# Part of a hybrid layer's elementwise work moved from VectorE and ScalarE to GpSimd

## The chip, the cores and the metric

The kernel runs on one core of a Trainium2 chip. The metric is the time of one execution on the device in microseconds (us). Five engines work side by side: TensorE (matrix products; PE in the rows, its weight loads PEld), VectorE (DVE), ScalarE (ACT), GpSimd (POOL) and SyncE (SP, which issues most transfers). Each has a queue of its own that it works off in order. TensorE's results land in PSUM, which GpSimd does not read in this kernel; all other tiles are in SBUF.

## The reference, cut to what matters

One layer of a streaming encoder runs over 512 tokens of a new stream and 64 tokens of a running one. Three of its steps matter here:

```
# state-space part, chunk by chunk
h_new = exp(last)[..., None, None] * h + einsum(w_end, x, Bk)      # decay of the state, then the update
y = (y + d_skip * xh).reshape(b, T, SSD_WIDTH) * silu(z)           # gating
y_ssd = rmsnorm(y, ssd_norm)
...
# attention part
s = where(mask, s * scale, -inf)
pr = softmax(s)                                                    # exp(s - max), divided by its sum
o = einsum(pr, keys_c) ...
x = x + concat([y_ssd, o]) @ w_out
# then a dense SwiGLU feed-forward layer
```

There are 8 state-space heads of 64 channels and 8 attention heads. All data is float32. Most products are made as three products of a high and a low half of each operand, so that many tiles come with a "high" copy (made by ScalarE) and a "low" difference (made by VectorE).

## The kernel before, in words

Tokens lie along the free dimension, channels along the 128 partitions. The work goes through input projections and convolution (to about 87 us of the profiled execution), the state-space chunks together with the gate projection and the first attention projections (87 to 144 us), attention with the first part of the output projection (144 to 218 us), the rest of the output projection (to 250 us) and then the feed-forward layer, which takes the rest.

The state-space part has five chunks: 0 to 3 of the new stream with 128 tokens each, and 4, of the running stream, with 64. `chunk_a` and `chunk_e` prepare a chunk (GpSimd's only arithmetic here is the select at line 515), `chunk_b` makes its output in the tile `xsd`, `chunk_s` the next running state `h`: a product of the old state with the decay `el` (line 569) and a sum with the update from PSUM (line 570). `gate` multiplies a chunk's part of `xsd` by `sz` (line 582); ScalarE squares the result (line 584), TensorE sums the squares over channels and ScalarE keeps the sums. When the sums of all chunks are there, `norm_y` and `cat_tile` (line 764, then `split_scaled`, lines 143 and 145) make the tiles `cat_y`, which the output projection takes.

Attention goes by pairs p of heads and blocks i of 128 queries (i = 4 is the running stream). `scores` makes a block's scores in PSUM; `soft` takes the maximum on VectorE (line 655), the exponential with its sum on ScalarE (line 656), the reciprocal of the sums on VectorE (line 657) and then scales the probabilities `pr`: head 0 of the pair on VectorE (line 662), head 1 on ScalarE (line 660). A block i of the new stream has (i + 1) x 128 keys. `turn` then transposes all blocks' probabilities through TensorE (line 694), and VectorE and ScalarE copy them back to SBUF. `pair_proj` issues, from GpSimd's queue, four transfers that bring a pair's rotary rows to the query buffer `qs` (line 616); pairs 2 and 3 reuse the buffers of pairs 0 and 1.

The order on each engine is written out: the strings `ORDER_...` give the order in which the steps are made, and the table `ISSUE` holds, for every engine, the order in which its instructions are issued, as numbers of the order in which they were made. `issue_in_order` puts it into effect. Nothing is reordered at run time.

Of the kernel before, what the change touches and what calls it, by code (L numbers as in the profile page):

```python
# [14 lines left out]
ALU = mybir.AluOpType  # L15
# [4 lines left out]
P = 128  # L20
# [34 lines left out]
def hybrid_layer_kernel(ctx: ExitStack, tc: tile.TileContext, a, o):  # L55
# [501 lines left out]
    def chunk_s(c):  # L557

        L, tk, ecp, el, xdt, bt, xw, wts = pre.pop(c)
        h = hT.pop(c)  # L560
        pst = bank("pp", f"ps_s{c}")
        for g in range(2):
            pe.matmul(pst[:, g * 256 : g * 256 + 256], bt[:L, g * P : g * P + P], xw[:L, g * 256 : g * 256 + 256], start=True, stop=True)
        hn = sd.tile([P, 512], F32, tag="hT", name=f"h_{c}", bufs=3)
        if h is None:
            act.copy(hn, pst)
        else:
            hv = lambda z: z.rearrange("p (h q) -> p h q", h=H)
            dve.tensor_tensor(hv(hn), hv(h), el.unsqueeze(2).to_broadcast([P, H, HD]), ALU.mult)
            dve.tensor_tensor(hn, hn, pst, ALU.add)  # L570
        if c == 4:
            sp.dma_start(o["ssm_sT"], hn)
        elif c == 3:
            sp.dma_start(o["ssm_pT"], hn)
        else:
            hT[c + 1] = hn

    def gate(c):
# [3 lines left out]
        dve.tensor_tensor(yv, yv, sz[:, :, tk], ALU.mult)  # L582
# [65 lines left out]
    def soft(p, i, scs, nk):  # L648
# [9 lines left out]
        for j in range(n):  # L658
            if j:
# [669 lines left out]
900-903 925-926 913-921 927-934 922-924 935 939-940 936-938 949-957 964-966 941 945-948 967-968 958-963 969 942-944
970-975 987 976-979 1003 980-986 991-993 988 1004-1005 1015-1021 1006-1014 1022-1024 994-996 1025-1026 1029-1034  # L1330
1043-1045 997-998 989 1000-1002 999 1046-1054 990 1035-1039 1059-1061 1040-1042 1062-1064 1027-1028 1075-1077
1081-1092 1055-1057 1078-1080 1093-1096 1058 1097-1104 1121-1123 1071-1072 1124-1129 1065 1068-1070 1073 1105-1107
1066-1067 1074 1130-1156 1119-1120 1229-1240 1157 1108-1114 1158 1241-1245 1253-1262 1246-1247 1115-1118 1159-1161
1176-1177 1248-1252 1263-1264 1162-1175 1265 1180 1178 1181-1183 1179 1266-1268 1277-1279 1184-1187 1190-1195
1269-1276 1196-1204 1188-1189 1205-1223 1227-1228 1224-1226 1280-1297 1301-1303 1298-1300 1304-1321 1342-1343
1348-1355 1344-1347 1322-1341 1356-1511 1572 1512-1559 1575-1576 1560-1571 1577 1596-1598 1578 1573-1574 1593
1584-1585 1579 1581-1583 1602-1604 1623-1625 1594-1595 1614 1586 1605-1606 1590-1592 1611-1613 1632-1634 1587-1589
1608-1610 1607 1580 1599-1601 1620-1622 1641 1626-1628 1647-1649 1642-1643 1615-1616 1635-1637 1617-1619 1638-1640
1653 1656 1658-1667 1644-1646 1629-1631 1650-1652 1654-1655 1668-1669 1657 1682 1694-1705 1683-1693 1670-1681
1730-1741 1706-1729 1742-1748 1754-1755 1749-1753 1756-1767 1778-1785 1768-1777 1786-1885 1898-1905 1886-1897  # L1340
1906-2017 2030-2036 2018-2029 2037-2053 2066-2084 2054-2065 2085-2089 2102-2104 2090-2101 2105-2221 2234-2236
2240-2241 2222-2233 2237 2242-2248 2238-2239 2249-2725 2738-2740 2744 2726-2737 2741 2745-2751 2742-2743 2752-3229
3242-3244 3248 3230-3241 3245 3249-3255 3246-3247 3256-3733 3746-3748 3752 3734-3745 3749 3753-3759 3750-3751
3760-4189
# [5 lines left out]
101-102 125 120 126-127 119 131-133 155 134 129 135-136 140-142 149 104 152 128 150 153 170 143-144 138 145 147 151  # L1350
154 156 137 146 174 157 178 159 171-172 187 169 160 158 161-162 176 206 163 175 183 180 164 167 165-166 168 215 181
177 188 173 189 182 184 190 195 191 179 192-194 197 185-186 224 196 204 207-209 198-203 214 205 210 288 211 225
216-218 212 220 222 219 213 226 221 223 227-228 233 229-230 234 231-232 235-236 245 255 246 237 294 256 247 239 248
257 259 258 260 240 238 264 241 261 242 263 262 307 267 243 265 244 266 249 268 270 251 269 253 250 274 252 254
275-276 289 271 290 277-279 295 286 280 282 281 287 272 297 317 291 283 318 273 298 302 299 316 300 284-285 319 303
306 292-293 296 309 312 304 326 305 310 308 313 327 362 311 328 322 301 323 314 363 330 324 320 329 315 336 321 325
364 333 367 337 331-332 365 340 338 334-335 341 344 349 339 350 345 342 346 352 351 343 355 358 366 347 359 357 348
360 356 353 361 368 377 354 370-371 369 372 375-376 373-374 382 390 378 384 383 385-386 379 389 387 380 397 388 381
393 405 395 391 396 394 392 400 399 401 398 403 402 420 406 404 408 407 409 412 410 417 414 411 413 418 462 416 421
423 419 464 425 422 424 415 433 431 426 432 429 428 427 438 430 434 469 463 436 435 437 439 442 441 443 466 440 444  # L1360
451 465 446 467-468 452-453 445 447 455 454 448 473 475 456 477 476 474 457 472 470 478 458-459 449-450 479 460 481
480 461 471 482 491 487 483 496-497 484 488 498-499 489 500-502 485-486 503 510 490 515-518 522 492 504 519 506 520
507 521 508 532-535 539 546 493-495 536 547-549 505 511-512 509 523 537 529-530 524-525 513-514 531 538 540 528 550
541 566 526 542 527 551 543 545 552 544 567-568 553-554 569 555 574 570 556-559 561 575-576 560 565 577 562 578-581
571 582-583 572 563 590-591 584 592 585-586 564 598 573 599-600 593-594 587-588 601 589 603 602 595 604-607 596 610
597 608-609 620-623 611 627 612 624 613-614 625-626 619 634-636 628 637 617 638 618 629 616 615 630 641 639 631 640
633 632 654-656 642 657 643 662 658 644-647 649 663-664 648 653 665 650 666-669 659 670-671 660 651 678-679 672 680
673-674 652 686 661 687-688 681-682 675-676 689 677 691 690 683 692-695 684 698 685 696-697 708-711 699 715 700 712
701-702 713-714 707 722-724 716 725 705 726 706 717 704 703 718 729 727 719 728 721 720 742-744 730 745 731 750 746
732-735 737 751-752 736 741 753 738 754-757 747 758-759 748 739 766-767 760 768 761-762 740 774 749 775-776 769-770  # L1370
763-764 777 765 779 778 771 780-783 772 786 773 784-785 796-799 787 803 788 800 789-790 801-802 795 810-812 804 813
793 814 794 805 792 791 806 817 815 807 816 809 808 830-832 818 833 819 839 834 820-823 825 840-841 824 829 842 826
843-846 835 847-848 836 827 855-856 849 857 850-851 828 864 837 865-866 858 838 859 852-853 867 854 869 868 860
870-873 861 876 862 874 880 875 881-883 887 884 863 885 877 886 879 878 888-898
""",
    "ACT": """
0-5 8 6-7 10 9 13 11 14 12 15 17-18 16 21 19 24 20 23 40 22 25 45 26-27 52 28-33 49-50 56 34-35 37 36 60 51 41-43
38-39 64 44 46-48 53-54 68 55 57-58 72 59 61-62 76 63 65-67 77 69-71 73 92 74-75 94 79 88 78 81 104 82 90 84 116 86-87
103 85 83 100 98 80 97 89 99 102 101 96 91 126 105 93 111 109-110 156 115 95 107-108 113 122 114 112 142 117 163 106
118-119 136 127 137 134 128 140 135 124 121 120 139 129 138 141 130 123 143 131 125 150 146 149 132 210 133 145 148  # L1380
154 152 151 147 158-159 157 144 155 160-162 153 164-165 212 170 172 171 166 168 180 186 169 181 174 187 175 173 176
189 167 190 177 227 178 192 179 193 188 182 195 194 191 183 200 196 184-185 199 201 197 213 208 215-216 202-203 219
209 204 217 234 218 198 205-206 211 214 226 220 233 221 240 207 223 242 224 222 241 229 243-244 225 271 235 230 228
231 238 237 272 232 245 236 248 239 246 249-252 247 257 255 261 254 262 256 259 263 258 278 265 253 267 266 264
268-270 260 273-277 284 280-282 285 287 283 279 293 286 291 288 290 289 302 292 294 296 295 298 300 297 301 303-304
# [123 lines left out]
```

## Time and profile before

| | before |
|---|---|
| median of 3 runs | 635.12 us (634.90 to 635.19) |
| profiled execution | 634.82 us, of which its span from first to last instruction is 633.1 us |
| granted TensorE clock, mean | 0.997 |
| TensorE busy | 622.9 us (98% of the span) |
| VectorE busy | 541.9 us (86%) |
| ScalarE busy | 400.0 us (63%) |
| GpSimd busy | 110.9 us (18%) |

The shares are averages over stages with different limits. A busy TensorE is not TensorE at its peak, since matrix products are pipelined and their ends are modelled; what holds the end is read from the chain of waits, which is followed back from the last instruction. Start times are counted from the first instruction of the span.

### The profile page before, as it was taken

How to read it: one execution, taken by the hardware profiler on the slowest of the kernel's cores; microseconds unless marked ns; L12 is line 12 of the kernel's file. 1: busy time of each engine (PE TensorE's matmuls, PEld its weight loads, DVE VectorE, ACT ScalarE, POOL GpSimd, SP SyncE). 2: the span in 40 equal slices, each digit the busy share in tenths (PEclk: the TensorE clock that was granted, in tenths of full speed). 3: DMA queues.
4: the chain of work that ended last, by engine and by line, in shares of the span. 5: the costliest groups of instructions: out<-in, count | busy, mean ns of one | idle time of the engine just before them, and what ended most of it. 6: DMA issues, size and time to landing. Idle time of an engine off the chain costs nothing.

```text
span 633.1 us, 12089 instructions
## 1 busy us (share of the span) xinstructions
PE 622.9 (98%) x4635; PEld 596.2 (94%) x4635; DVE 541.9 (86%) x945; ACT 400.0 (63%) x768; POOL 110.9 (18%) x164
## 2 busy tenths in 40 slices
PE   9999999999999999999999999999999999999995
PEld 8899999886787899999999999999999999999995
DVE  6999986899776699999999888988899789976555
ACT  7655346779775567666556676566656665767364
POOL 1322103001010000001301330033104220323323
PEclk9999999999999999999999999999999999999998
DMA  8322364323231223335743986398738893689924
GB/s 320 135 61 74 96 198 122 113 75 102 81 117 34 95 73 126 88 113 172 260 131 89 217 182 156 79 191 186 172 100 161 198 204 101 101 215 256 254 38 149
DMA packets 39593, 89.19 MB, mean 141 GB/s; under 512 B 4570, under 2 KB 14312, under 8 KB 39280
## 3 DMA queue, kind: packets, MB, share of 16 engines
q1 hardware_dynamic: 26416, 63.12, 30.9%
q0 software_dynamic: 12400, 24.73, 21.4%
q8 instruction: 36, 0.59, 0.4%
q10 hardware_dynamic: 720, 0.57, 0.3%
q14 instruction: 21, 0.17, 0.1%
HBM read 62.74 MB, written 24.53 MB: 138 GB/s over the span
## 4 chain that ended last, share of the span: by engine, by line
PE 90%; DVE 5%; ACT 2%; issue 1%; POOL 1%; DMA 1%; POOLq 0%; DVEq 0%
PE ps_x L874 21%; PE ps_d L1064 14%; PE ps_z L874 10%; PE ps_in L281 8%; PE ps_o L458 5%; PE ps_y L874 5%; PE ps_z L458 4%; PE ps_first L129 3%; PE ps_d L281 2%; PE ps_p L874 2%; PE ps_l L281 2%; PE sc L672 2%; PE pv L719 1%; PE ptp L694 1%; PE ps_q L458 1%
## 5 line engine op out<-in xcount | busy, mean ns | idle before, releaser
L874 PE MATMUL ps_x<-xop,wh_gu_S 128*128 128x288 f32 x378 | 76.9, 295 | 0.0
L112 DVE TENSOR_TENSOR wl_gu_S<-gu,wh_gu_S 128x1024 fp32r<-128x1024 f32 x44 | 53.3, 1220 | 9.7 <-ACT wh_gu_S L111 6.5
L874 PEld LDWEIGHTS ps_x<-xop,wh_gu_S 128*128 128x128 f32 x378 | 60.5, 188 | 0.0
L1078 POOL DMA_DIRECT2D acc<-fz x32 | 27.9, 904 | 165.2 <-ACT fz L1075 136.5
L111 ACT CAST wh_gu_S<-gu 128x1024 fp32r<-128x1024 f32 x44 | 46.3, 1052 | 16.2 <-PE ps_y L874 8.3
L874 PE MATMUL ps_x<-xop,wl_gu_S 128*128 128x288 f32 x189 | 55.8, 295 | 0.0
L281 PE MATMUL ps_in<-xs,wh_in 128*128 128x256 f32 (+1 forms) x256 | 51.2, 296 | 0.4 <-DVE sp_a L361 0.4
L281 PEld LDWEIGHTS ps_in<-xs,wh_in 128*128 128x128 f32 x256 | 40.8, 188 | 1.2 <-issue 1.1
L281 PE MATMUL ps_in<-xs,wl_in 128*128 128x320 f32 (+1 forms) x128 | 37.7, 295 | 0.0
L874 PEld LDWEIGHTS ps_x<-xop,wl_gu_S 128*128 128x128 f32 x189 | 35.5, 188 | 0.0
L111 ACT CAST wh_gu_A<-gu 128x1024 fp32r<-128x1024 f32 x22 | 23.1, 1050 | 10.3 <-PE ps_x L874 6.9
L874 PE MATMUL ps_z<-xop,gu_a 128*128 128x288 f32 x189 | 29.5, 294 | 0.0
L458 PE MATMUL ps_o<-cat_y,wh_out 128*128 128x256 f32 (+1 forms) x128 | 29.0, 312 | 0.3 <-DVE cat_y L145 0.3
L112 DVE TENSOR_TENSOR wl_gu_A<-gu,wh_gu_A 128x1024 fp32r<-128x1024 f32 x22 | 26.8, 1218 | 1.2 <-ACT wh_gu_A L111 1.0
L874 PE MATMUL ps_x<-xop_last,wh_gu_S 128*128 128x288 f32 x126 | 26.9, 295 | 0.0
L874 PEld LDWEIGHTS ps_z<-xop,gu_a 128*128 128x128 f32 x189 | 26.5, 188 | 0.0
L1064 PE MATMUL ps_d<-pair,d_1h 128*128 128x288 f32 x128 | 26.4, 296 | 0.0
L874 PE MATMUL ps_z<-xop,wh_gu_S 128*128 128x288 f32 x126 | 26.0, 295 | 0.0
L458 PE MATMUL ps_z<-xs,wh_z 128*128 128x256 f32 (+1 forms) x128 | 25.8, 296 | 0.1
L458 PE MATMUL ps_o<-cat_o,wh_out 128*128 128x320 f32 (+1 forms) x128 | 25.5, 295 | 0.3 <-DVE x L750 0.3
L874 PE MATMUL ps_y<-xop,wh_gu_A 128*128 128x288 f32 x126 | 25.8, 296 | 0.0
L874 PE MATMUL ps_x<-xop,wh_gu_A 128*128 128x288 f32 x126 | 25.7, 295 | 0.0
(417 smaller groups left out, 2138.9 us busy)
## 6 DMA issues: line engine op xcount, KB each, us to landing
gu<-in_w_gu SPq DMA_DIRECT2D x44, 512.0 KB, 5.5
wr_d<-in_w_down SPq DMA_DIRECT2D x18, 512.0 KB, 4.0
acc<-fz POOLq DMA_DIRECT2D x16, 288.0 KB, 6.8
acc<-da POOLq DMA_DIRECT2D x16, 288.0 KB, 8.1
acc<-dc POOLq DMA_DIRECT2D x16, 288.0 KB, 8.6
wr_in<-in_w_in SPq DMA_DIRECT2D x8, 512.0 KB, 3.7
wr_out<-in_w_out SPq DMA_DIRECT2D x8, 512.0 KB, 3.3
cumb<-cumD SPq DMA_DIRECT2D x5, 512.0 KB, 4.5
```

Of the source, the lines that this page charges most:

```text
L111: act.copy(hi, raw)
L112: dve.tensor_tensor(lo, raw, hi.bitcast(F32), ALU.subtract)
L129: pe.matmul(ps[:m, hf, : cols.stop - cols.start], w, x[:, cols], start=start and k == 0 and i == 0, stop=stop and k == last and i == 2,)
L281: pe.matmul(ps, w, x[:, cols], start=first and k == 0 and i == 0, stop=last and k == len(terms) - 1 and i == 2,)
L458: pe.matmul(ps[:, :n], w, x[:, cols], start=k == 0 and i == 0, stop=k == len(terms) - 1 and i == 2,)
L672: pe.matmul(s[:, :nk], qs[:, j, q0 : q0 + P], ks[:, j, :nk], start=True, stop=True)
L694: pe.transpose(pp[:, k : k + P], prs[p, i][:, j, b * P : b * P + P], ident)
L719: pe.matmul(pv[64 * j : 64 * j + 64, b * P :], V[b][:, h * HD : (h + 1) * HD], pts[p, b, j], start=b == 0, stop=True, skip_group_check=b > 0,)
L874: pe.matmul(ps, p, q, start=not onto and first and kp == kps[0] and j == 0, stop=onto or (last and kp == kps[-1] and j == 2), skip_group_c ...
L1064: pe.matmul(ps, p, v, start=not onto and n == 0 and j == 0, stop=onto or (n == len(ks) - 1 and j == 2), skip_group_check=onto,)
L1078: pool.dma_start(out, src, accum_op=ALU.add)
```

## The change

Three kinds of instructions are issued to GpSimd instead of VectorE or ScalarE; what is computed stays the same. The decay of the state in chunks 1 to 3 (chunk 0 has none, chunk 4 stays on VectorE); the gating of chunks 4, 0 and 1 (2 and 3 stay); and the scaling of the probabilities of head pair 0 for its four blocks of the new stream, both heads, so four instructions of VectorE and four of ScalarE. The orders of VectorE, ScalarE and GpSimd are written anew for the new numbers; those of TensorE and SyncE stay.

```diff
@@ chunk_s
-            dve.tensor_tensor(hv(hn), hv(h), el.unsqueeze(2).to_broadcast([P, H, HD]), ALU.mult)
+            (dve if c == 4 else pool).tensor_tensor(hv(hn), hv(h), el.unsqueeze(2).to_broadcast([P, H, HD]), ALU.mult)
             dve.tensor_tensor(hn, hn, pst, ALU.add)
@@ gate
-        dve.tensor_tensor(yv, yv, sz[:, :, tk], ALU.mult)
+        (pool if c in (4, 0, 1) else dve).tensor_tensor(yv, yv, sz[:, :, tk], ALU.mult)
@@ soft
         for j in range(n):
-            if j:
+            if p == 0 and i < 4:
+                pool.tensor_scalar(pr[:, j], pr[:, j], sm[:, j : j + 1], None, ALU.mult)
+            elif j:
                 act.activation(pr[:, j], pr[:, j], AF.Identity, scale=sm[:, j : j + 1])
             else:
                 dve.tensor_scalar(pr[:, j], pr[:, j], sm[:, j : j + 1], None, ALU.mult)
@@ ISSUE, "POOL" (its first lines)
-0-3 7 18 28 4 8 5 9 6 10 26 11 27 12 29 13-17 20-23 19 24-25 31 30 32-42 53 55 57 59 54 56 58 60 43-52 61-69 71 73 75
+0-3 7 18 28 4 8 5 9 6 10 26 11 27 12 29 13-17 20-23 19 24-25 31 30 32-42 57 59 61 63 58 60 62 64 43-48 52-54 49-51 55-56
+65-83 85 87 89 84 91 93 95 88 90 86 97 92 94 96 98-101 103 102 104 106 105 107-117 119 118 120 122 121 123-133 135 134
...
```

In GpSimd's new list 49, 50 and 56 are the gatings of chunks 4, 0 and 1; 51, 65 and 66 the decays of chunks 1, 2 and 3; 67 to 74 the eight scalings, in the order of the blocks 3, 1, 2, 0; and 75 to 82 the transfers for pairs 2 and 3. The lists of VectorE and ScalarE are the old ones without the ten and the four instructions that left, with the rest renumbered.

## Rows read from the trace of the kernel before

**Rows 1.** Busy time by stretch: length, PE, PEld, DVE, ACT, POOL (instructions), clock, DMA.

```profile
118.00:143.00 25.00, 25.00 (x195) 21.77 (x195) 23.77 (x48) 19.76 (x48) 1.09 (x1) 1.00 0.21 63
143.00:160.65 17.65, 15.96 (x81) 10.59 (x80) 17.34 (x42) 16.20 (x45) 1.96 (x4) 1.00 0.39 130
```

**Rows 2.** Chain that ended last: start, length, engine, tile, line.

```profile
143.02 0.32 DVE h L570
143.34 0.61 DVE ecp L554
...
150.39 0.26 DVE pr L662
...
153.14 0.16 DVE pr L662
...
155.19 0.20 DVE pr L662
...
159.93 0.68 DVE cat_y L145
```

**Rows 3.** Removed instructions: by line (ns min/median/max), then grouped (busy us, mean ns).

```profile
L569 DVE TENSOR_TENSOR h<-h,el x3: 679/683/685, 125.5 to 141.5; 128x512 f32<-128x512 f32 x3
...
L582 DVE TENSOR_TENSOR xsd<-xsd,sz x5: 427/691/691, 120.6 to 145.3; 128x512 f32<-128x512 f32 x4, 128x256 f32<-128x256 f32 x1
...
L662 DVE TENSOR_SCALAR pr<-pr,sm 128x512 f32<-128x512 f32 (+3 forms) x4 | 1.5, 378 | 0.0
...
L660 ACT ACTIVATE pr<-pr,sm 128x256 f32<-128x256 f32 (+3 forms) x4 | 2.0, 556 | 0.0
```

**Rows 4.** GpSimd's arithmetic grouped by line and form (busy us, mean ns); a copy.

```profile
L1271 POOL TENSOR_TENSOR fz<-fz,sq 128x256 f32<-128x256 f32 x7 | 5.2, 738 | 5.5 <-ACT sq L1266 5.0
...
L515 POOL TENSOR_SCALAR_AFFINE_SELECT cumb<-cumb 128x1024 f32<-128x1024 f32 x4 | 4.4, 1092 | 25.2 <-ACT el L490 25.2
...
57.61 0.19 POOL L398 COPY nconv<-up 128x3 f32<-128x3 f32 x1
```

**Rows 5.** Timeline of VectorE and GpSimd where they overlap: start, length, instruction.

```profile
114.86 1.09 POOL L515 TENSOR_SCALAR_AFFINE_SELECT cumb<-cumb 128x1024 f32<-128x1024 f32 x1 [5.28 <-ACT el L490]
...
115.20 1.36 DVE L472 SCALAR_TENSOR_TENSOR sz<-zt,zh 128x576 f32<-128x576 f32 x1
...
119.80 0.75 DVE L472 SCALAR_TENSOR_TENSOR sz<-zt,zh 128x576 f32<-128x576 f32 x1
...
47.76 1.35 DVE L319 TENSOR_TENSOR cq<-cq,Rq 128x1152 f32<-128x1152 f32 x1
...
48.00 1.16 POOL L397 COPY nconv<-up 128x3 f32<-128x3 f32 x1
```

**Rows 6.** Timeline near the end: two-input sums on both engines.

```profile
611.01 1.02 POOL L1222 TENSOR_TENSOR fz<-fz,sq 128x320 f32<-128x320 f32 x1
...
611.94 0.49 DVE L1227 TENSOR_TENSOR sq_last<-sq_last,sq 128x320 f32<-128x320 f32 x1
...
613.23 0.48 DVE L1227 TENSOR_TENSOR sq_last<-sq_last,sq 128x320 f32<-128x320 f32 x1
```

**Rows 7.** VectorE's groups from 149 to 156.3 us that read two SBUF tiles.

```profile
L179 DVE SCALAR_TENSOR_TENSOR Ry<-nr_u,nr_y 128x288 f32<-128x288 f32 x2 | 0.9, 454 | 0.0
L178 DVE TENSOR_TENSOR nr_u<-nr_u,nr_v 128x288 f32<-128x288 f32 x2 | 0.9, 446 | 0.0
L764 DVE SCALAR_TENSOR_TENSOR xsd<-xsd,par,Ry 128x576 f32<-128x576 f32 x1 | 0.8, 812 | 0.0
...
L112 DVE TENSOR_TENSOR wl_pair<-wr_pair,wh_pair 128x384 fp32r<-128x384 f32 x1 | 0.6, 550 | 0.0
```

**Rows 8.** Timeline: pair 2's transfers, pair 0's first turns, pair 2's first scores.

```profile
153.06 2.02 POOL L616 DMA_DIRECT2D qs<-rrp  x4 [24.56 <-PE sc_s L678]
...
156.63 0.60 PE L694 MATMUL ptp<-ident,pr 128*128 128x128 f32 x4
...
173.71 0.59 PE L672 MATMUL sc<-ks,qs 100*128 100x512 f32 x1
```

More of the change, by code (lines that the diff above doesn't have):

```diff
@@ L1329 @@
[L1329 to L1338, printed above, removed]
@@ L1344 @@
-3760-4189
+98-99 93-97 70-73 86-91 104-106 100-103 110 107-109 122-126 134-135 111-115 128-133 148-153 116-121 136-141 127 142-147
+154-169 174-175 170-171 270-274 176-221 172-173 222-269 275-370 373-420 371 421-468 372 469-634 637 641-644 638-640
+657-660 635-636 665-726 737-758 661-664 763 645-652 759-760 727-736 764-766 653-656 767-818 859 761-762 819-826 860-864
+833-840 827-832 865-870 841-852 871-874 853-856 875-880 857-858 881-887 904-912 888 892-899 889-891 900-903 925-926
+913-921 927-934 922-924 935 939-940 936-938 949-957 964-966 941 945-948 967-968 958-963 969 942-944 970-975 987 976-979
@@ new lines @@
+1003 980-986 991-993 988 1004-1005 1015-1021 1006-1014 1022-1024 994-996 1025-1026 1029-1034 1043-1045 997-998 989
+1000-1002 999 1046-1054 990 1035-1039 1059-1061 1040-1042 1062-1064 1027-1028 1075-1077 1081-1092 1055-1057 1078-1080
+1093-1096 1058 1097-1104 1121-1123 1071-1072 1124-1129 1065 1068-1070 1073 1105-1107 1066-1067 1074 1130-1156 1119-1120
+1229-1240 1157 1108-1114 1158 1241-1245 1253-1262 1246-1247 1115-1118 1159-1161 1176-1177 1248-1252 1263-1264 1162-1175
+1265 1180 1178 1181-1183 1179 1266-1268 1277-1279 1184-1187 1190-1195 1269-1276 1196-1204 1188-1189 1205-1223 1227-1228
@@ new lines @@
+1224-1226 1280-1297 1301-1303 1298-1300 1304-1321 1342-1343 1348-1355 1344-1347 1322-1341 1356-1511 1572 1512-1559
+1575-1576 1560-1571 1577 1596-1598 1578 1573-1574 1593 1584-1585 1579 1581-1583 1602-1604 1623-1625 1594-1595 1614 1586
+1605-1606 1590-1592 1611-1613 1632-1634 1587-1589 1608-1610 1607 1580 1599-1601 1620-1622 1641 1626-1628 1647-1649
+1642-1643 1615-1616 1635-1637 1617-1619 1638-1640 1653 1656 1658-1667 1644-1646 1629-1631 1650-1652 1654-1655 1668-1669
+1657 1682 1694-1705 1683-1693 1670-1681 1730-1741 1706-1729 1742-1748 1754-1755 1749-1753 1756-1767 1778-1785 1768-1777
@@ L1345 @@
+1786-1885 1898-1905 1886-1897 1906-2017 2030-2036 2018-2029 2037-2053 2066-2084 2054-2065 2085-2089 2102-2104 2090-2101
+2105-2221 2234-2236 2240-2241 2222-2233 2237 2242-2248 2238-2239 2249-2725 2738-2740 2744 2726-2737 2741 2745-2751
+2742-2743 2752-3229 3242-3244 3248 3230-3241 3245 3249-3255 3246-3247 3256-3733 3746-3748 3752 3734-3745 3749 3753-3759
+3750-3751 3760-4189
 """,
@@ L1374 @@
-870-873 861 876 862 874 880 875 881-883 887 884 863 885 877 886 879 878 888-898
+101-102 125 120 126-127 119 131-133 155 134 129 135-136 140-142 149 104 152 128 150 153 170 143-144 138 145 147 151 154
+156 137 146 174 157 178 159 171-172 187 169 160 158 161-162 176 203 163 175 183 180 164 167 165-166 168 211 181 177 188
+173 189 182 184 190-191 179 192-194 185-186 220 195 204-206 196-202 207 278 208 212-214 209 216 218 215 210 221 217 219
+222-225 228 226-227 229-230 239 248 240 231 284 249 241 233 250-252 234 232 255 235 253 236 254 297 257 237 256 238 242
@@ new lines @@
+258 260 244 259 246 243 264 245 247 265-266 279 261 280 267-269 285 276 270 272 271 277 262 287 307 281 273 308 263 288
+292 289 306 290 274-275 309 293 296 282-283 286 299 302 294 316 295 300 298 303 317 352 301 318 312 291 313 304 353 320
+314 310 319 305 326 311 315 354 323 357 327 321-322 355 330 328 324-325 331 334 339 329 340 335 332 336 342 341 333 345
+348 356 337 349 347 338 350 346 343 351 358 367 344 360-361 359 362 365-366 363-364 372 380 368 374 373 375-376 369 379
+377 370 387 378 371 383 395 385 381 386 384 382 390 389 391 388 393 392 410 396 394 398 397 399 402 400 407 404 401 403
@@ new lines @@
+408 452 406 411 413 409 454 415 412 414 405 423 421 416 422 419 418 417 428 420 424 459 453 426 425 427 429 432 431 433
+456 430 434 441 455 436 457-458 442-443 435 437 445 444 438 463 465 446 467 466 464 447 462 460 468 448-449 439-440 469
+450 471 470 451 461 472 481 477 473 486-487 474 478 488-489 479 490-492 475-476 493 500 480 505-508 512 482 494 509 496
+510 497 511 498 522-525 529 536 483-485 526 537-539 495 501-502 499 513 527 519-520 514-515 503-504 521 528 530 518 540
+531 556 516 532 517 541 533 535 542 534 557-558 543-544 559 545 564 560 546-549 551 565-566 550 555 567 552 568-571 561
@@ new lines @@
+572-573 562 553 580-581 574 582 575-576 554 588 563 589-590 583-584 577-578 591 579 593 592 585 594-597 586 600 587
+598-599 610-613 601 617 602 614 603-604 615-616 609 624-626 618 627 607 628 608 619 606 605 620 631 629 621 630 623 622
+644-646 632 647 633 652 648 634-637 639 653-654 638 643 655 640 656-659 649 660-661 650 641 668-669 662 670 663-664 642
+676 651 677-678 671-672 665-666 679 667 681 680 673 682-685 674 688 675 686-687 698-701 689 705 690 702 691-692 703-704
+697 712-714 706 715 695 716 696 707 694 693 708 719 717 709 718 711 710 732-734 720 735 721 740 736 722-725 727 741-742
@@ new lines @@
+726 731 743 728 744-747 737 748-749 738 729 756-757 750 758 751-752 730 764 739 765-766 759-760 753-754 767 755 769 768
+761 770-773 762 776 763 774-775 786-789 777 793 778 790 779-780 791-792 785 800-802 794 803 783 804 784 795 782 781 796
+807 805 797 806 799 798 820-822 808 823 809 829 824 810-813 815 830-831 814 819 832 816 833-836 825 837-838 826 817
+845-846 839 847 840-841 818 854 827 855-856 848 828 849 842-843 857 844 859 858 850 860-863 851 866 852 864 870 865
+871-873 877 874 853 875 867 876 869 868 878-888
@@ L1397 @@
-626 645 650 627 651 647-648 646 649 659-660 652 668-669 655-657 653 658 661 670 663 671 664-665 662 666-667 672
-677-678 654 679 675 673-674 676 680-682 684 683 685-687
+0-5 8 6-7 10 9 13 11 14 12 15 17-18 16 21 19 24 20 23 40 22 25 45 26-27 52 28-33 49-50 56 34-35 37 36 60 51 41-43 38-39
+64 44 46-48 53-54 68 55 57-58 72 59 61-62 76 63 65-67 77 69-71 73 92 74-75 94 79 88 78 81 104 82 90 84 116 86-87 103 85
+83 100 98 80 97 89 99 102 101 96 91 126 105 93 111 109-110 156 115 95 107-108 113 122 114 112 142 117 163 106 118-119
@@ new lines @@
+136 127 137 134 128 140 135 124 121 120 139 129 138 141 130 123 143 131 125 150 146 149 132 206 133 145 148 154 152 151
+147 158-159 157 144 155 160-162 153 164-165 208 170 172 171 166 168 180 185 169 181 174 186 175 173 176 187 167 188 177
+223 178 189 179 190-191 182 196 192 183-184 195 197 193 209 204 211-212 198-199 215 205 200 213 230 214 194 201-202 207
+210 222 216 229 217 236 203 219 238 220 218 237 225 239-240 221 267 231 226 224 227 234 233 268 228 241 232 244 235 242
+245-248 243 253 251 257 250 258 252 255 259 254 274 261 249 263 262 260 264-266 256 269-273 280 276-278 281 283 279 275
@@ new lines @@
+289 282 287 284 286 285 298 288 290 292 291 294 296 293 297 299-300 295 305 301-302 306 303 308 325 304 307 312-313
+309-311 326 314 327 315-316 328 332 317-321 329 333 331 330 322 334 336 335 323 342 339 324 340 351-352 337-338 343-344
+353 345 354 346 359 348 347 349 341 350 368 355 369 356-357 370-371 378-379 360-366 380 367 372 358 377 381 376 382 373
+375 374 386-388 384 383 385 389 397 390 398 391 396 393 395 392 405 394 406 399 414-415 401-404 407 416 409 417 410-411
+408 412-413 400 418 423 420 424 419 421-422 431-432 425 440-441 427-429 426 430 433 442 434 443 436-437 435 438-439 444
@@ new lines @@
+452-453 445 454 446 450 447 451 449 448 455 460 456 461-462 458 457 459 463 471 464 472 465 470 467 469 466 479 468 480
+473 488-489 475-478 481 490 483 491 484-485 482 486-487 474 492 497 494 498 493 495-496 505-506 499 514-515 501-503 500
+504 507 516 508 517 510-511 509 512-513 518 526-527 519 528 520 524 521 525 523 522 529 534 530 535-536 532 531 533 537
+545 538 546 539 544 541 543 540 553 542 554 547 562-563 549-552 555 564 557 565 558-559 556 560-561 548 566 571 568 572
+567 569-570 579-580 573 588-589 575-577 574 578 581 590 582 591 584-585 583 586-587 592 600-601 593 602 594 598 595 599
@@ L1399 @@
+597 596 603 608 604 609-610 606 605 607 611 619 612 620 613 618 615 617 614 628 616 629 621 637-638 624-627 630 639 632
+640 633-634 631 635-636 622 641 646 623 647 643-644 642 645 655-656 648 664-665 651-653 649 654 657 666 659 667 660-661
+658 662-663 668 673-674 650 675 671 669-670 672 676-678 680 679 681-683
 """,
     "POOL": """
[L1401 to L1402 removed]
@@ L1408 @@
+67 65 76 69-71 78 73 86 64 74-75 87 80 88-89 84 90 85 91 98 101 99-100 102-103 106-165
 """,
```

59 lines of the change are left out of this document (2 added, 57 removed).

## The prediction

> **What bounds the kernel now.** The change lies in two neighbouring stretches, so I read the busy times of those first. From 118 to 143 us TensorE is busy for all 25.00 us, VectorE for 23.77 and ScalarE for 19.76; from 143 to 160.65 us TensorE drops to 15.96 of 17.65 us while VectorE has 17.34 and ScalarE 16.20 [rows 1]. The reader is to see two regimes: first TensorE has no gap, and help for another engine is worth nothing there; then VectorE and ScalarE hold TensorE up, and there help can pay. GpSimd is nearly idle in both (1.09 and 1.96 us).
>
> The chain of waits says the same more sharply [rows 2]. It runs through TensorE up to 143 us, changes to VectorE with the last piece of h at line 570 (0.32 us), and then goes through VectorE and ScalarE until the low half of cat_y is written (159.93 us, 0.68 us long); from 160.65 us it is TensorE's again. So a stretch of some 17.6 us is set by VectorE and ScalarE, and only what shortens that passage shortens the kernel. Three of the scalings that the change takes away stand in the chain themselves, with 0.26, 0.16 and 0.20 us.
>
> The orders written out for VectorE and ScalarE are, after renumbering, the old ones with the ten and the four removed instructions left out: nothing else moves on those two engines. TensorE's and SyncE's lists are unchanged.
>
> **Gatings and decays (six instructions).** VectorE loses three decays of about 0.68 us and three gatings of 0.69, 0.69 and 0.43 us, 3.85 us in all [rows 3]. GpSimd gains them at its own price. The nearest rows are its two-input products and sums of 256 columns at 0.738 us and a copy of three columns at 0.19 us [rows 4]; the slope is (738 - 190) / 256 = 2.14 ns a column, so 512 columns cost about 0.19 + 1.10 = 1.29 us (an estimate), and six of them 5 x 1.29 + 0.74 = 7.2 us. Lower bound: VectorE's own 3.85 us; upper bound: as estimated plus as much again by interference, some 11 us. They are spread over 120 to 142 us, where GpSimd has room for either. Each ends 0.3 to 0.6 us later than it would on VectorE if it starts at the same time, but the decays need not wait for VectorE's turn any more and start earlier. What hides all of this is TensorE without a gap up to 143 us. Behind the gating of a chunk ScalarE's square waits, and the rest of ScalarE's queue; if that cover were gone, each of the three gatings could cost its extra 0.6, together 1.5 us with the short one.
>
> What is gained is the end of the stretch: the last decay (0.68 us on VectorE) stands just ahead of the final state update and of the product with ecp at line 554. With it gone VectorE reaches line 570 before the 0.32 us piece shown in the chain, and line 554 then waits for TensorE alone instead. Of the 0.32 us I take 0.25; bounds 0 and 0.32.
>
> **Scalings of pair 0 (eight instructions).** VectorE loses four, 1.5 us; ScalarE loses four, 2.0 us [rows 3]. In the chain VectorE's share is 0.26 + 0.16 + 0.20 = 0.62 us [rows 2]; the fourth, of 512 columns, lies where ScalarE is the later one and I count nothing for it. ScalarE's four lie after its last piece on the chain and count nothing by themselves; they keep ScalarE from becoming the next bound when VectorE runs ahead.
>
> GpSimd does 2 x (512 + 256 + 384 + 128) = 2560 columns. No tensor-by-scalar product of GpSimd stands in the trace. Lower rate: its one-input select over 1024 columns, 1.09 us, less the 0.19 us, is 0.88 ns a column; eight instructions then take 8 x 0.19 + 2560 x 0.88 ns = 3.8 us. Upper rate: two inputs, 8 x 0.19 + 2560 x 2.14 ns = 7.0 us [rows 4]. I take 3.8, because the scaling too reads one tensor. Its start is given by the reciprocals on VectorE, so it can't begin before about 149 us; the first turns of pair 0 on TensorE begin at 156.63 us [rows 8]. 149 + 3.8 is early, 149 + 7.0 = 156.0 is barely in time.
>
> **What the two engines do to each other.** A select of GpSimd began at 114.86 us and ran 1.09 us; VectorE's product of two SBUF tensors that began at 115.20 took 1.36 us, against 0.75 us of the same instruction elsewhere: it ended 0.61 us after the select did, as if it had begun its work only then. The other way, a GpSimd copy of three columns took 1.16 us while VectorE's 1.35 us product of two SBUF tensors ran [rows 5]. But a GpSimd sum with two inputs behaves otherwise: during it VectorE's two-input sum took 0.49 us, against 0.48 us without it, and the GpSimd sum itself stretched to 1.02 us [rows 6].
>
> The Trainium skill, "SBUF — State Buffer", section "Who interferes with whom", says that a VectorE instruction with two SBUF inputs and a GpSimd instruction that reads SBUF exclude each other for a whole instruction, whichever starts first; this speaks against the change. The select agrees with that rule; the two-input sum does not. By the rule all eight scalings block VectorE, and the sum is the one below, near nothing; if they behave as in [rows 6] it is the rival that gives way, 0.87 us better.
>
> For the scalings I follow the select, the one-input form. Between 149 and 156.3 us VectorE has two instructions each of lines 178 and 179, one of line 112 and the first of line 764, all with two SBUF inputs: 0.9 + 0.9 + 0.6 + 0.8 = 3.2 us [rows 7]. By the order of the queue three meet a scaling: the first line 178 meets those of 256 columns (0.42 us each), line 112 those of 384 (0.53), line 179 or 764 those of 128 (0.30). Each meeting costs between half and one whole scaling, so 0.6 to 1.25 us; I take 0.7. It falls on VectorE inside the chain.
>
> **A queue that is passed.** The four DMA issues that fetch the rotary rows of pair 2 stood first in GpSimd's queue at 153.06 us (2.02 us) and now stand behind all eight scalings, so after some 155 to 160 us. Their scores begin on TensorE at 173.71 us [rows 8]: more than 10 us of cover, so I cost this at nothing; without the cover it would be the 3 to 7 us of the delay.
>
> **The sum.** -0.25 (line 554) - 0.62 (three scalings) + 0.70 (VectorE kept waiting) = -0.17 us. The profiled execution took 634.82 us, span 633.1 and 1.7 around it, which is 0.3 below the median of 635.12; its forecast is 634.65, and for the median of runs 635.12 - 0.17, about 634.9 us. A difference below 0.2% (1.3 us) can hardly be told from no change here.
>
> **Rivals.**
> *The scalings give way to VectorE, as the two-input sum did.* Then 0.25 + 0.62 = 0.87 us stays: 634.25. The two-input sum [rows 6] speaks for it, the select [rows 5] against.
> *The scalings are slow and late.* At 7.0 us, and each also held up by VectorE's 3.2 us of two-input work, they end at 149 + 7.0 + 3.2 = 159.2 us, 2.6 us after TensorE's first turns want them; ScalarE's copy of these turns then holds the next high halves of cat_y behind it. That decides from about 7.6 us for the eight together, when they come after the 156.63 us. Price +1.5 to +3: 636.6 to 638. For it: no such instruction was measured. Against it: one input, and the select's rate.
> *The gatings hold ScalarE.* The three gatings' 1.5 us come through in part, +0.3 to +0.9: 635.4 to 636. Against it: TensorE's full cover [rows 1].
> *The relief is worth more than the chain shows.* TensorE's missing time from 143 to 160.65 us is 17.65 - 15.96 = 1.69 us [rows 1]. If all of it came back together with the 0.25, 633.2. For it: ScalarE's 2.0 us. Against it: TensorE's waits there are behind score exponentials that ScalarE makes before any of its removed instructions.
>
> **How the numbers follow.** Forecast (634.3 to 635.4): 0.44. Giving way: 0.21. Slow and late: 0.20. Gatings hold ScalarE: 0.07. Worth more: 0.08. The likeliest gives 634.9. With 1.3 us as the border, the last case is the faster one, 0.08; the slow one is slower in nearly all of its width, and with the edge of the gating case I put 0.21; 0.71 remains for the same. The range leaves out half of the slow case's upper part and the case worth more: 634.0 to 637.0.
>
> **What would show it.** Right: scalings of about 0.6, 0.5, 0.4 and 0.3 us on GpSimd; one or two VectorE instructions of lines 178, 112, 179 or 764 longer by 0.2 to 0.6 us; TensorE taking the chain back at about 160.4 us; line 554 beginning some 0.2 us earlier. Wrong: scalings of 1.2 us or more for 512 columns, first turns after 157 us, a TensorE gap before 143 us, or ScalarE's squares waiting for GpSimd for over half a microsecond.

## The result, and the profile after

The changed kernel takes 638.28 us, median of six runs (636.29 to 638.65), against 635.15 us of the kernel before in the same session (634.9 to 635.39): a ratio of 1.0042, with a 95% interval from 1.0027 to 1.0057 (ratios are estimated from all executions, not from the two medians). The forecast was 634.9 us in a range up to 637.0. It was wrong: the kernel became slower by 3 us, and the rival "the scalings are slow and late" came true, at a time above its upper price.

The six times fall into two groups, 636.3 and 636.8 us, and 638.1 to 638.7 us. The profile of the changed kernel is of the first group (636.29 us, span 634.4, against 633.1 before); a profile of the second came with the first experiments.

The busy times by stretch, columns as in [rows 1], in the changed kernel:

```profile
118.00:143.00 25.00, 25.00 (x195) 21.77 (x195) 21.00 (x42) 19.95 (x49) 7.91 (x7) 1.00 0.21 62
143.00:160.65 17.65, 15.69 (x74) 10.10 (x73) 16.10 (x37) 13.25 (x39) 11.40 (x11) 0.90 0.34 125
```

Up to 143 us all is as forecast: TensorE has no gap, VectorE is down from 23.77 to 21.00 us. Behind it VectorE and ScalarE did get their relief (16.10 for 17.34 us, 13.25 for 16.20), but GpSimd works 11.40 of 17.65 us, and the granted clock is 0.90 where it was 1.00.

GpSimd's instructions of the changed kernel grouped by line and form, from 118 to 160 us:

```profile
L569 POOL TENSOR_TENSOR h<-h,el 128x512 f32<-128x512 f32 x3 | 3.5, 1171 | 8.2 <-DVE h L570 6.3 <-ACT h L566 1.8
L660 POOL TENSOR_SCALAR pr<-pr,sm 128x512 f32<-128x512 f32 x2 | 3.4, 1698 | 7.8 <-DVE sm L657 7.8
L660 POOL TENSOR_SCALAR pr<-pr,sm 128x384 f32<-128x384 f32 x2 | 2.7, 1362 | 0.0
L582 POOL TENSOR_TENSOR xsd<-xsd,sz 128x512 f32<-128x512 f32 x2 | 2.6, 1279 | 3.4 <-DVE xsd L555 2.5 <-DVE xsd L547 0.9
L660 POOL TENSOR_SCALAR pr<-pr,sm 128x128 f32<-128x128 f32 x2 | 2.2, 1131 | 0.0
L660 POOL TENSOR_SCALAR pr<-pr,sm 128x256 f32<-128x256 f32 x2 | 1.9, 942 | 0.0
...
L582 POOL TENSOR_TENSOR xsd<-xsd,sz 128x256 f32<-128x256 f32 x1 | 0.7, 744 | 4.7 <-DVE sz L472 4.7
```

All seven rows are moved work. The gatings cost 1.28 and 0.74 us, as estimated. The eight scalings cost 3.4 + 2.7 + 2.2 + 1.9 = 10.2 us, where 3.8 was taken and 7.0 was thought to be the upper bound. After the first they wait in GpSimd's queue for nothing else (idle before 0.0): GpSimd itself is the bound.

What that does is in the chain of waits (start, length, what), the part that answers to the end of [rows 2]:

```profile
150.82 4.18 POOL pr L660 x4
...
157.15 2.25 POOL pr L660 x2
159.40 0.04 issue
159.45 0.66 PE ptp L696 x4
...
161.40 2.72 PE ps_o L458 x21
```

and in the timelines of ScalarE, then of TensorE (first turns and pair 2's scores):

```profile
158.71 0.59 ACT L698 COPY pt<-ptp 128x512 f32<-128x512 f32 x1 [2.10 <-PE ptp L696]
...
159.87 1.83 ACT L143 ACTIVATE cat_y<-xsd 128x576 fp32r<-128x576 f32 x3
```

```profile
158.02 0.66 PE L696 MATMUL ptp<-ident,pr 128*128 128x128 f32 x4
...
174.90 1.45 PE L674 MATMUL sc<-ks,qs 100*128 100x512 f32 x3
```

GpSimd stands in the chain with 6.5 us, where it was absent. The first turn begins at 158.02 us instead of 156.63, the second at 159.45. ScalarE waits 2.10 us to copy the first, and the high halves of cat_y stand behind that copy in its queue. TensorE's long products resume at 161.40 us instead of 160.65 with 21 matmuls still to do where there were 15, and pair 2's scores, [rows 8], begin 1.19 us later (174.90 for 173.71). The span grew by 1.3 us: in this execution that shift is nearly all of the loss.

The other 2 us of the higher group are TensorE's clock, as far as its profile shows. Busy times in four stretches of 4 us, columns as above (the clock is the third figure from the end), first of the kernel before, then of the changed kernel in the profile above, then of the changed kernel in a slower execution (638.9 us, span 637.0):

```profile
150.00:154.00 4.00, 2.85 (x17) 1.75 (x16) 3.94 (x13) 3.96 (x15) 0.92 (x2) 1.00 0.08 30
154.00:158.00 4.00, 3.77 (x16) 1.91 (x15) 4.00 (x11) 3.93 (x11) 1.04 (x3) 1.00 0.86 263
```

```profile
154.00:158.00 4.00, 3.87 (x6) 1.28 (x4) 3.96 (x9) 1.36 (x5) 4.00 (x5) 0.57 0.85 308
158.00:162.00 4.00, 3.33 (x23) 2.86 (x24) 3.18 (x6) 3.12 (x7) 3.38 (x5) 1.00 0.44 155
162.00:166.00 4.00, 4.00 (x31) 3.93 (x30) 3.51 (x9) 1.19 (x4) 0.00 (x0) 1.00 0.03 6
```

```profile
154.00:158.00 4.00, 2.15 (x7) 0.96 (x7) 3.96 (x9) 1.12 (x3) 4.00 (x5) 1.00 0.93 339
158.00:162.00 4.00, 3.35 (x16) 2.85 (x15) 3.19 (x6) 3.13 (x7) 3.14 (x5) 0.57 0.39 129
162.00:166.00 4.00, 4.00 (x19) 3.66 (x18) 1.03 (x2) 0.00 (x0) 0.00 (x0) 0.58 0.00 1
```

In the faster execution the clock is near its lower level (1.2 GHz) from 154 to 158 us, while TensorE would wait for GpSimd anyway, so the slow scores hide in that wait. In the slower one TensorE runs through them at full clock, then idles for 1.85 us in front of the first turn (2.15 of 4 us busy), and the clock is down from 158 to 166 us, when the turns and the long products set the time. The chain of that execution:

```profile
159.21 1.12 PE ptp L696 x4
...
162.88 3.91 PE ps_o L458 x21
```

1.12 and 3.91 us for 0.66 and 2.72 us; with the pieces between (0.64, 0.64 and 1.28 for 0.33, 0.33 and 0.65) that is 7.59 for 4.69 us, 2.9 us more, against a span 2.6 us longer.

The difference between 2.9 and 2.6 us lies ahead of all this. The executions are not equally far when the passage begins, by up to 1.1 us between those profiled, so a start time in one trace is only roughly comparable with one in another. What can be compared is the length of the passage: here, from the start of TensorE's last products of line 553 to the start of pair 0's first products with the values (`pv`), both from the chain. Before, changed kernel, slower execution:

```profile
142.31 0.68 PE ps_i L553 x6
...
167.95 2.08 PE pv L719 x10
```

```profile
142.34 0.67 PE ps_i L553 x6
...
169.14 2.08 PE pv L721 x10
```

```profile
142.11 0.67 PE ps_i L553 x6
...
171.81 2.08 PE pv L721 x10
```

The passage takes 25.64 us before, 26.80 us in the first profile of the changed kernel (1.16 more) and 29.70 us in the second (4.06 more).

### The profile page after: what moved, and what is told of

It reads as the page before. It is cut to its first block, busy times and chain, and to the rows that moved or that the text cites. A ratio compares the mean times of both kernels' runs of the same rounds, so it can differ in the third digit from the quotient of the medians.

```text
span 634.4 us, 12100 instructions
## 1 busy us (share of the span) xinstructions
PE 623.5 (98%) x4635; PEld 596.2 (94%) x4635; DVE 538.3 (85%) x935; ACT 398.1 (63%) x764; POOL 128.1 (20%) x178
## 4 chain that ended last, share of the span: by engine, by line
PE 89%; DVE 3%; ACT 2%; POOL 2%; issue 2%; DMA 1%; POOLq 0%; DVEq 0%; ACTq 0%
PE ps_x L876 21%; PE ps_d L1066 14%; PE ps_z L876 10%; PE ps_in L281 8%; PE ps_y L876 5%; PE ps_o L458 4%; PE ps_z L458 4%; PE ps_first L129 3%; PE ps_d L281 2%; PE sc L674 2%; PE ps_p L876 2%; PE ps_l L281 2%; PE pv L721 1%; PE ptp L696 1%; POOL pr L660 1%
## 5 line engine op out<-in xcount | busy, mean ns | idle before, releaser
L1025 POOL DMA_DIRECT2D acc<-dn x8 | 4.4, 544 | 121.6 <-ACT dn L1024 121.6
```

## The experiments

All kernels are variants of the changed one or of the one before; VectorE's and ScalarE's order lists are those of before with the moved instructions left out. The edits are cut to the lines that matter and written in a short form. "The passage" is the length defined above, from each run's own profile.

**Gatings and decays alone, scalings alone.** The first keeps the old line for the scalings; the second has

```diff
-(dve if c == 4 else pool).tensor_tensor(hv(hn), ...)
+dve.tensor_tensor(hv(hn), ...)
-(pool if c in (4, 0, 1) else dve).tensor_tensor(yv, ...)
+dve.tensor_tensor(yv, ...)
```

> Only the three gatings and the three decays on GpSimd; all eight scalings stay on VectorE and ScalarE. Theory A (the eight scalings, 10.14 us in a row on GpSimd, end too late for the first turns; all of the loss comes from them): 634.6 to 635.0 us, TensorE without a gap to 143 us and first turns at 156.4 to 156.7 us. Rival B (the gatings and decays, 1.0 to 1.4 us each instead of 0.7, cost by holding ScalarE's squares or by blocking VectorE's long products): 635.5 to 638 us, with a share of the loss seen here.

> Only the eight scalings on GpSimd; gatings and decays stay on VectorE. Theory A: the whole loss, 636.3 to 638.7 us, with scalings of 1.3 to 1.8 us for 512 columns, first turns at about 158 us and TensorE's granted clock at half for some microseconds before them. Rival B: 634.9 to 635.5 us.

Measured: 635.05 us (634.71 to 635.3; ratio 0.9998, 0.999 to 1.0007), just above theory A's 635.0 and under rival B's 635.5, and 638.14 us (638.04 to 638.39; ratio 1.0049, 1.0036 to 1.0063). The gatings and decays cost nothing and give nothing that can be measured in the time (the passage is 0.18 us shorter, 25.46 us); the scalings alone are the whole loss. In the second kernel's timeline of GpSimd they take the same time from a start that is a microsecond later, as this whole execution is (its last products of line 553 start at 143.17 us):

```profile
150.18 10.14 POOL L660 TENSOR_SCALAR pr<-pr,sm 128x512 f32<-128x512 f32 x8 [20.82 <-DVE nr_v L173]
```

Its passage takes 28.07 us, 2.43 more than before: the same lateness, and some 1.2 us of low clock. The clock fell later than theory A had it, behind the start of the first turn (158.96 us) and not ahead of it: it is 1.00 from 154 to 158 us, 0.67 from 158 to 162 us and 0.91 from 162 to 166 us. So this kernel's 638.14 us is put together otherwise than the 638.9 us above.

**The first four scalings only.**

```diff
-if p == 0 and i < 4:
+if p == 0 and i in (1, 3):
```

> Gatings, decays and the first four scalings (512, 512, 256 and 256 columns) on GpSimd; the last four (384, 384, 128, 128) stay on VectorE and ScalarE. Theory A: the four end at about 154.5 us, before any turn wants them; nothing is late, 634.4 to 635.0 us. Rival C (a scaling on GpSimd costs by what it takes from VectorE while both run, wherever it lies): about half of the loss, 636 to 637 us, with VectorE's instructions of lines 173, 178, 179 and 112 longer. Rival D (TensorE's clock falls because of the thin work from 151 to 158 us, not because of late turns): the clock at half here too.

Measured: 635.59 us (634.86 to 636.11; ratio 1.0005, 0.9997 to 1.0014), which is no difference from before, though above the interval that theory A gave. Its scalings take 1.57, 1.82, 0.98 and 1.03 us and end at 154.63 us; the turns are not late and the clock stays at 1.00 from 150 to 166 us. So it isn't the slow scaling as such that costs, but that eight in a row end after they are wanted. Rivals C and D fall in this execution. The gain is small: the passage takes 25.47 us for 25.64. The profiled execution takes 635.92 us all the same, with a span 1.0 us longer than before. That comes at the very end, where the two kernels do the same: there the clock is 0.73 from 624 to 628 us, against 1.00 in the profile before.

**The changed kernel again.**

> The changed kernel once more, unaltered: its six times fell into two groups, 636.3 to 636.8 and 638.1 to 638.7 us. If the profile comes from the higher group, its trace shows where the other 2 us are: by theory A in the stretch from 150 to 165 us (turns later still, or the clock at half for longer); by rival E in another part of the kernel, such as the later products, by a lower clock there.

Measured: 638.27 us (638.09 to 638.9; ratio 1.0053, 1.004 to 1.0065). Its profile is the third window table above: this execution of the higher group has its 2 us in the stretch from 158 to 166 us, and E falls. No other of that group was profiled.

**TensorE kept busy in its idle time.** Before the turns of pair 0, into their own PSUM bank:

```diff
+for _ in range((10, 3)[j] if p == b0 == 0 else 0):
+    pe.matmul(pp[:, :P], ones, ones, start=True, stop=True)
```

> The changed kernel with 13 more 128-column products of ones on TensorE, into the bank of the first turns, before it is used: three ahead of the long scores near 152.8 us, seven ahead of the first turn, three ahead of the second; their results are overwritten. Theory F (the loss has two parts: turns some 1.3 us late, and on top TensorE's granted clock at half for 4 to 7 us after the idle time that the late turns leave): the clock stays at 1.00 from 150 to 166 us and 636.0 to 636.8 us are left, in one group. Rival G (the clock is not what parts the two groups, or such products don't keep it up): 638 us or more, with the clock at half in the same place.

> The kernel with the 13 products of ones once more: its seven times lay between 636.25 and 637.83 us, while its one profile, at 636.26 us, had the clock at 1.00 all through. Theory F: a profile above 637 us shows the clock at half somewhere between 150 and 166 us for 2 to 4 us, so the products kept it up only in some executions. Rival G: the clock is at 1.00 there, and the missing microsecond lies elsewhere.

Measured: 637.14 us (636.25 to 637.83; ratio 1.0032, 1.0021 to 1.0043), and in the second session 636.39 us (636.07 to 637.59; ratio 1.0018, 1.0008 to 1.0027). The windows of the first profile (636.26 us):

```profile
154.00:158.00 4.00, 3.77 (x20) 2.48 (x18) 3.96 (x9) 1.40 (x5) 4.00 (x5) 1.00 0.85 315
158.00:162.00 4.00, 3.94 (x29) 3.50 (x30) 3.19 (x6) 3.13 (x7) 3.42 (x6) 1.00 0.40 141
```

The clock is at 1.00 all through, in the second profile (636.74 us) too, and the turns are as late as in the changed kernel. The passage takes 26.81 us in both: what is left at full clock is the lateness alone, some 1.2 us. In the first profile of the changed kernel it took 26.80 us, so the low clock from 154 to 158 us had cost nothing there. The two sessions lie 1 to 2 us under the changed kernel, so the clock is a real part of the loss. Theory F's one group at 636.0 to 636.8 us did not come: seven of these 17 times lie above it, five of them above 637 us, and no profile caught one of those five. In one, 637.47 us, the mean granted clock over the whole execution is 0.999, as high as in any run, so there it can hardly have been the clock; for the others it is open.

**What a scaling costs by itself.** On the kernel before, 23 instructions on a scratch tile of GpSimd's own, four kinds:

```diff
+pool.tensor_scalar(scr[:, :n], scr[:, :n], ones[:, :1], None, ALU.mult)
+pool.tensor_scalar(scr[:, :n], scr[:, :n], 1.0, None, ALU.mult)
+pool.tensor_tensor(scr[:, :n], scr[:, :n], ones[:, :1].to_broadcast([P, n]), ALU.mult)
+pool.tensor_copy(scr[:, :n], scr[:, :n])
```

> The kernel before, with 23 instructions more on GpSimd behind the last pair's rotary rows (from about 180 us), on a scratch tile that nothing else reads: scalings by a column (512, 256 and 128 columns), scalings by a constant, products with a broadcast column (two inputs) and copies. Theory H (the scaling by a column itself is the slow thing: about 0.24 us and 2.6 ns a column): 1.5 to 1.6 us for 512 columns and 0.55 to 0.60 us for 128, with nothing beside it; the product with two inputs 1.2 to 1.35 us. Rival I (the scalings were slow by VectorE's work beside them): 0.65 to 0.8 us for 512 columns here.

The kernel took 636.15 us in its only run. Measured, grouped by line and form (the four lines are 622, 624, 626, 628):

```profile
L622 POOL TENSOR_SCALAR scr<-scr,ones 128x512 f32<-128x512 f32 x3 | 4.7, 1571 | 0.3
L624 POOL TENSOR_SCALAR scr<-scr 128x512 f32<-128x512 f32 x3 | 4.5, 1511 | 0.3
L626 POOL TENSOR_TENSOR scr<-scr,ones 128x512 f32<-128x512 f32 x3 | 4.0, 1328 | 0.2
...
L622 POOL TENSOR_SCALAR scr<-scr,ones 128x256 f32<-128x256 f32 x2 | 1.9, 926 | 0.2
L628 POOL COPY scr<-scr 128x512 f32<-128x512 f32 x3 | 1.8, 615 | 0.2
L624 POOL TENSOR_SCALAR scr<-scr 128x128 f32<-128x128 f32 x2 | 1.1, 531 | 0.2
L626 POOL TENSOR_TENSOR scr<-scr,ones 128x128 f32<-128x128 f32 x2 | 0.8, 401 | 0.2
```

and the one 128-column scaling by a column with no long product of VectorE beside it, in the timeline (the other took 1.61 us beside a 1.23 us product of line 112):

```profile
188.44 0.60 POOL L622 TENSOR_SCALAR scr<-scr,ones 128x128 f32<-128x128 f32 x1
```

Theory H holds and I falls. A scaling of 512 columns takes 1.57 us with nothing heavy beside it, by a constant hardly less (1.51). The copy, which also reads one tensor, takes 0.615 us. The slopes from 128 to 512 columns: scaling (1.571 - 0.60) / 384 = 2.5 ns a column, copy (0.615 - 0.297) / 384 = 0.83 ns, with 0.297 us for the copy of 128 columns. The product with two inputs is cheaper than the scaling, and cheaper than the 1.2 us expected: two of its three took 1.04 us; the third, 1.90 us, met VectorE's 1.26 us product of line 112. So the eight scalings alone would take 2 x (1.571 + 1.249 + 0.926 + 0.60) = 8.7 us (1.249 for 384 columns is the mean of its neighbours), and the 10.14 us hold about 1.4 us of waiting beside VectorE.

Up to the added instructions this kernel is the kernel before, and still TensorE's clock is 0.57 from 154 to 158 us in this profile. The passage takes 26.17 us, 0.53 more.

**The scalings as products with two inputs.**

```diff
-pool.tensor_scalar(pr[:, j], pr[:, j], sm[:, j : j + 1], None, ALU.mult)
+pool.tensor_tensor(pr[:, j], pr[:, j], sm[:, j : j + 1].to_broadcast([P, nk]), ALU.mult)
```

> The changed kernel with the eight scalings written as products with two inputs, the second a broadcast column. If the two-input price of the decays (about 1.05 to 1.3 us for 512 columns) holds for it, the eight take 7 to 8.5 us instead of 10.1, the first turns come at 156.8 to 157.5 us, and the time lies at 635.2 to 636.5 us; if it is as slow as the scaling, 636.3 to 638.7 us.

Measured: 636.16 us (635.35 to 637.07; ratio 1.0017, 1.0008 to 1.0025). The eight take 7.0 us, the upper rate of the prediction, the first turn comes at 156.78 us, and two thirds of the loss are gone. The passage is still 0.90 us longer than before (26.54 us), at a clock of 1.00. About half of that comes from VectorE, in its groups from 149 to 157.5 us:

```profile
L178 DVE TENSOR_TENSOR nr_u<-nr_u,nr_v 128x288 f32<-128x288 f32 x2 | 1.5, 732 | 0.0
...
L112 DVE TENSOR_TENSOR wl_pair<-wr_pair,wh_pair 128x384 fp32r<-128x384 f32 x1 | 1.0, 987 | 0.0
```

0.732 and 0.987 us for 0.446 and 0.550 [rows 7]: now VectorE is held too, and the first low half of cat_y is ready 0.5 us later in the passage. GpSimd waits as well:

```profile
L660 POOL TENSOR_TENSOR pr<-pr,sm 128x384 f32<-128x384 f32 x2 | 1.9, 984 | 0.5 <-DVE sm L657 0.5
L660 POOL TENSOR_TENSOR pr<-pr,sm 128x128 f32<-128x128 f32 x2 | 1.5, 754 | 0.5 <-DVE sm L657 0.5
```

0.754 us for 128 columns where it took 0.40 on the scratch tile. By the prices of the scratch tile the eight would take 2 x (1.04 + 0.83 + 0.61 + 0.40) = 5.8 us (an estimate; 384 and 256 columns by the slope between 512 and 128), so 1.2 of the 7.0 us are waiting. The rest of the longer passage is the first sum with x (line 752), which waits 0.52 us for the load of x; the next experiment looks at that load.

**Only VectorE's four scalings, and then the next wait.** ScalarE keeps its four:

```diff
-if p == 0 and i < 4:
+if p == 0 and i < 4 and j == 0:
```

> Gatings, decays and the four scalings that VectorE had (512, 256, 384, 128 columns) on GpSimd; ScalarE keeps its four. By theory A and the measured prices each ends before its turn (the last at about 155.9 us against 156.6): nothing late, VectorE 0.5 to 0.8 us less in the passage that it bounds, 634.2 to 634.9 us, a version at least as fast as the kernel before. If GpSimd's scaling costs VectorE as much as it takes off, 635.0 to 635.6 us.

Measured: 635.25 us (634.75 to 637.48; ratio 1.0005, 0.9996 to 1.0014). Each scaling ended before its turn (the last at 155.6 us), yet nothing was gained, and the time lies in the interval of the second forecast, that the scalings cost VectorE what they take off it. The chain of waits shows another thing in the way:

```profile
154.28 9.06 DMA x<-in_xT
...
163.43 0.43 DVE x L752
```

The first sum with x waited 1.0 us for the load of x, and TensorE behind it; the passage takes 26.04 us, 0.40 more than before. In the kernel before the same load was issued at 154.3 us and took 8.2 us, so it landed at 162.5 us, just before VectorE came to it at 162.65: with the load in that place the passage could not have become much shorter in any case. So the load was taken forward in SyncE's queue, in this kernel and, as a control, in the kernel before:

```diff
 SP: ... 88
-89 84
+84 89
```

> As the kernel with gatings, decays and VectorE's four scalings on GpSimd, and in SyncE's queue the load of x (1152 KB) stands ahead of that of the second output weight (512 KB) instead of behind it. Theory J (what VectorE gains in the passage is given back at the next wait: the first sum with x waited 1.0 us for that load, which landed at 163.4 us, and TensorE behind it 0.5 us): x lands before 162 us, no gap of TensorE at 163 us, 634.3 to 634.9 us. Rival K (the passage itself gained nothing): 635.0 to 635.5 us.

> The kernel before with the same exchange in SyncE's queue, as a control. There x landed at 162.5 us, about 0.1 us before VectorE came to it. Theory J: nothing waits for it yet, so 634.9 to 635.3 us, no change. Rival K: if this alone gives 0.4 us or more, the load held the kernel before too.

Measured: 635.01 us (634.26 to 635.97; ratio 0.9994, 0.9985 to 1.0003) and 635.54 us (634.7 to 636.0; ratio 1.0, 0.9991 to 1.0009). In the first x is issued at 149.6 us and takes 5.9 us, and the wait is gone. Its passage takes 25.20 us, 0.44 less than before, which speaks for J against K; but the time lies at the edge of K's interval, and the gain that J gave it can't be told from none. The control's profile holds something else, in its windows and in its chain:

```profile
154.00:158.00 4.00, 4.00 (x7) 1.65 (x7) 4.00 (x12) 3.31 (x10) 1.14 (x3) 0.57 0.59 171
```

```profile
153.80 4.33 PE sc L674 x6
```

TensorE's clock is near the lower level, and six scores take 4.33 us, with no scaling on GpSimd at all. The passage takes 26.14 us, 0.50 more than before; here the low clock is not hidden, since no late scaling is waited for. So the fall of the clock after the thin work near 153 us needs no late turn: from 150 to 154 us TensorE was busy for 2.84 us here and for 2.85 us in the kernel before, whose clock stayed at 1.00 in its profile.

**A try at a better version.** The kernel with four scalings and x first, with three products of ones near 153.5 us:

> The kernel with gatings, decays and VectorE's four scalings on GpSimd and x loaded first, and three products of ones on TensorE in its idle time near 153.5 us, as a try for a version that beats the kernel before. Theory F: TensorE's clock stays at 1.00 from 150 to 166 us in all executions, which takes off the upper times of the kernel without them (634.26 to 635.97 us): median 634.3 to 634.8 us, highest below 635.5. Rival G: no change, 635.0 us with the same spread.

Measured: 634.76 us (634.25 to 635.73; ratio 0.9992, 0.9983 to 1.0001). The highest time is above the 635.5 us of theory F. The clock is at 1.00 from 150 to 166 us in its profile, and the passage takes 25.22 us, 0.42 less than before. It is the lowest median of all, 0.6 us under the kernel before in the same session (635.33), but its interval still touches 1: no version is shown to beat it.

## Why the prediction was wrong

**The bound** was read rightly: TensorE gapless to 143 us, VectorE and ScalarE after it. So were **the gatings and decays**: 1.28 and 0.74 us as estimated, 1.04 us for two decays and 1.42 for the third, all hidden. The 0.25 us at line 554 came to 0.15 us in the trace (it begins at 143.11 us for 143.26), and the passage with the gatings and decays alone is 0.18 us shorter; in the time that can't be told from nothing, and in the changed kernel the loss of the scalings covers it.

**The step that failed** is the price of the scalings: "I take 3.8, because the scaling too reads one tensor." They took 10.14 us, 8.7 of it their own. The select and the copy do run near 0.85 ns a column, but the scaling runs at 2.5: here the number of tensors read did not tell GpSimd's rate. The range failed with it, since a two-input product was called the upper rate and is cheaper than the scaling. The Trainium skill, "GPSIMD Engine Reference", section "4.1 Engine selection", calls instructions with one input on GpSimd roughly line-rate; the copy agrees with that here and the scaling does not, and the measurement decides.

**The lock** was put on VectorE at 0.70 us. VectorE's line 112 began 0.30 us into a scaling of 0.96 us (152.92 and 152.62 us), took 0.63 for 0.55 us and was done before it. VectorE lost most in the first product of line 766 (764 before), 1.02 for 0.81 us. It was mostly GpSimd that waited, 1.4 us in all. The Trainium skill, "SBUF — State Buffer", section "Who interferes with whom", lets the two engines exclude each other for whole instructions; line 112 ending inside a scaling disagrees with that; where GpSimd's two-input form held VectorE, the trace agrees more nearly.

**The queue that is passed** cost nothing, as said: pair 2's scores are late by the 1.19 us of everything else.

**The rival "slow and late"** had the mechanism down to its place: it put the last scaling's end at 159.2 us (159.39 by the trace) and named the copy that holds the high halves of cat_y. That the end came out within 0.2 us is partly luck: it was made of 7.0 us of scalings and 3.2 us of waiting, where the runs have 8.7 and 1.4. Its border of 7.6 us lies below the scalings' own 8.7. Its chance was too small, and both ends of its price were off, as it left out the clock, which stands in no term of the prediction: the lateness alone costs some 1.2 us, less than the lower price of 1.5, and the fall of TensorE's clock behind the idle time up to 2.9 more, according to whether it meets work that sets the time. **The forecast gain** was not there to be had either: with four scalings moved and nothing late, the load of x took its place. With x loaded first the passage is 0.44 us shorter in the profile, half of the 0.87 us that the prediction counted before the lock, and the times cannot tell even that from nothing.

What stays open: what decides in which execution the clock falls and for how long, and where the times above 637 us with TensorE kept busy come from. That the clock makes up the upper group of the changed kernel rests on one profile of that group.

## What to carry to other kernels

Price an operation on another engine by that operation: a select, a copy and a product on the same engine bound nothing when the scaling is dearer than all of them, and one run with a few of them on a scratch tile settles it. Ask first when each result is wanted, as four slow scalings cost nothing and eight cost 3 us (1.2 of them by being late, the rest by the clock in the executions where it fell then). And where a passage is to be shortened, look for the transfer that lands just before its end: here it was the next bound.

## What the runs showed of the hardware

- GpSimd's scaling by a column (1.57 us for 512 columns, 0.60 for 128) is slower than its product with two inputs (1.04 and 0.40 us), and a constant in place of the column hardly helps (1.51 and 0.53 us).
- The form of GpSimd's work changes who waits: beside the scaling it was mostly GpSimd (10.14 us for 8.7, with VectorE's line 112 at 0.63 us for 0.55), beside the two-input product GpSimd (7.0 us for an estimated 5.8) and VectorE too (0.73 us for 0.45, and line 112 at 0.99 us for 0.55).
- TensorE's granted clock falls to its lower level for some 3 to 7 us after a stretch of thin work, in some executions and not in others with the same program, and what it costs depends on what is waited for then: from 154 to 158 us nothing where TensorE had to wait for GpSimd anyway and 0.5 us in the kernel before (26.17 us of passage for 25.64), from 158 to 166 us 2.9 us.
